# Recasting the scan of a hybrid RWKV-7 layer: row-half products, a written matmul order, a solve in pieces

## The chip, the cores and the metric

The kernel runs on one core of a Trainium2 chip. The metric is the device time of one execution in microseconds, as the median over runs; lower is better. The engines are TensorE (PE in the profile, with its weight loads as PEld), VectorE (DVE), ScalarE (ACT), GpSimd (POOL) and SyncE (SP), which issues the DMA transfers here.

## The reference, cut to what matters

One layer: a SwiGLU block, a token mixer, and a second SwiGLU block, each followed by a LayerNorm. 1152 tokens (128 of context, 1024 latent) of 1024 channels, in f32. The change touches the token mixer's recurrence, which runs forward and backward over the tokens for 16 heads of 64 channels:

```python
def _rwkv7_step(S, inp):
    r, w, k, v, kk, a = inp
    sa = jnp.einsum('dbhvk,dbhk->dbhv', S, kk)
    S = S * w[..., None, :] - sa[..., :, None] * (kk * a)[..., None, :] + v[..., :, None] * k[..., None, :]
    return S, jnp.einsum('dbhvk,dbhk->dbhv', S, r)
```

The outputs y of both directions are added, normalised over the 64 channels of each head (the group norm), joined by a bonus term, gated and projected. A second branch pools the tokens over windows, and two sigmoid gates weigh the branches. The final context states are an output too.

## The kernel before, in words

**The stages.** `tile_step` runs the first SwiGLU block; the input projection of the mixer with all that prepares the scan; the scan; then the output projections and the second SwiGLU block. The big products work on 384 tokens at a time with 128x128 weights, each value split into two fp32r parts, three matmuls for a product (`mm3`, lines 134 to 136). `Weights.get` loads a weight (line 122), ACT casts its high part (line 125), and DVE or POOL subtracts for the low part (line 127).

**The scan.** It treats 64 tokens as a chunk. The 18 chunks of 8 heads are a pass of 18 steps, the first two of context, and there are two passes (`hb`): 36 steps in `steps`. A step handles one chunk of the forward direction (d = 0) and one of the backward direction (d = 1) at once. Inside a step the recurrence becomes small f32 products, in `main(s)`:

- line 1015: the state times the chunk's keys and queries, into `xy`. Two heads share 128 partitions. The state is kept twice: `Sc`, plain, [128, 4, 64], and `Sb`, block diagonal, [128, 4, 128], so that one product with 128 rows serves two heads. One step has eight such products.
- line 1020: adds the masked products `LM` times the values, for the half of `xy` that holds x (d = 0 in partitions 0 to 63, d = 1 in 64 to 127).
- line 1024: ACT copies x to `Xs`, a half for each direction.
- line 1028: the inverse `W` of a triangular matrix times `Xs`; line 1032: ACT writes minus the result into `vu`, beside the values.
- line 1038: the update of the state, `sp`; line 1039 (DVE) adds it to `Sc`, line 1040 (POOL) multiplies by the decay, and lines 1041 and 1042 (ACT) copy the two halves into `Sb`.
- line 1046: the outputs y; line 1049 copies them to `yt`, and they go to a tile of the group norm or to memory.

Ahead of a step, `pre` loads its chunk `ak` (512 KB for a direction, three buffers), `pre_lm` computes the masks' products (line 987, one row half `e` at a time, four products of 64 rows, then a DVE multiply by the mask, line 988), and `pre_kb` transposes the keys (line 994).

**The solve.** `solve(i)` inverts the triangular matrices of four steps (two units). It loads them (lines 735 and 737), copies one of them transposed on ACT (line 739), runs 31 dependent pairs of DVE operations (lines 744 and 746), sends the result through memory to rearrange it (line 748 and after), transposes on DVE (lines 755, 758), and joins the 32-wide blocks by small matmuls (line 768, `ph`). The inverse is written to memory (`wi_d`, line 781) and read back by `load` into `W`. Solve 0 runs before the scan; the others start at every fourth step, for the unit two solves ahead; the head of a solve is emitted in one go, its four matmul parts one at a time.

**The filler.** The projections of the gates and of the pooling branch, 900 matmuls of 384 columns, are a generator, `filler`. Sixty of them (`AHEAD`) run before the first step; `fill(k)` emits the rest in five places of each step, in the shares of `SPREAD`.

**The group norm.** `group_norm(hb, tt)` is emitted when both directions of 128 tokens are there: a sum on POOL (line 1081), mean, subtraction, squares, variance, power and product on DVE, ACT and POOL (lines 1083 to 1091). `back` then transposes on TensorE (line 1096), scales on ACT (line 1100), adds the bonus on POOL (line 1101) and stores. The parts left at the end of the scan run inside the next stage, in `w_o`.

**What sets the order.** The compiler's scheduler orders the instructions of each engine by a simulated timeline, the earlier in the program the higher the priority. `tc.manual_schedule(engines=...)` keeps the program's order for the named engines instead; the opening, the ends of the SwiGLU blocks and the output projections have it for TensorE. In the scan before, the scheduler also orders TensorE, except that `tc.issue_after` holds the filler and the solve's matmuls behind a named matmul of the step.

Of the kernel before, what the change touches and what calls it, by code (L numbers as in the profile page):

```python
# [11 lines left out]
ALU = mybir.AluOpType  # L12
# [9 lines left out]
SPREAD = (7, 7, 6, 6, 0)  # L22
# [38 lines left out]
def tile_step(ctx: ExitStack, tc: tile.TileContext, I: dict, O: dict):  # L61
# [40 lines left out]
    wi_d = [dram.tile([P, 16, 64], F32, name=f"wi_{u}") for u in range(18)]  # L102
# [470 lines left out]
    with pool("mp", 4, psum=True) as psum, pool("ma", 2, psum=True) as paux, \  # L573
# [137 lines left out]
        gn = ctx.enter_context(pool("gn"))  # L711
# [9 lines left out]
        Wb = [sv.tile([P, 32, 64], F32, name="Wb0")]  # L721
        G.memset(Wb[0], 0.0)

        def solve(i, pps):
            def t4(nm):
                return sv.tile([P, 32, 32], F32, name=nm, tag="sv", bufs=4)
            Gq, Gt, Nt = t4("Gq"), t4("Gt"), sv.tile([P, 32, 32], F32, name="Nt")
            for k in range(2):
                u = 2 * i + k
                for d in range(2):  # L730
                    c0 = chunk0(u, d)
                    cb, cc, hb = c0 // 6, c0 % 6, u // 9
                    for hf in range(2):
                        p0 = d * 64 + hf * 32 + k * 16
                        S.dma_start((Gt if d else Gq)[p0:p0 + 16], qd_d[d][hb][cb][hf][:, cc:cc + 2].rearrange("a c e s t -> a (c e) (s t)"))
                    r0 = 96 * d
                    S.dma_start(Nt[r0:r0 + 32, k * 16:k * 16 + 16].rearrange("s (a n) t -> s a (n t)", a=4),
                                nd_d[d][hb][cb][:, :, cc:cc + 2].rearrange("s a c e t -> s a (c e t)"))
            A.copy(Gq[64:128], Gt[64:128].rearrange("p s t -> p t s"))
            Wd, pr = t4("Wd"), t4("pr")  # L740
            S.dma_start(Wd, I["id32"])
            for k in range(31):
# [3 lines left out]
                V.tensor_tensor(Wd[:, 0:k + 1, k + 1:32], Wd[:, 0:k + 1, k + 1:32], o, ALU.subtract)  # L746
            ed = dram.tile([2, 2, 32, 32, 32], F32, name="ed", tag="ed", bufs=2)
            S.dma_start(ed.rearrange("d b n i t -> (d b n) i t"), Wd)
            W = Wb[0]
            Dx = t4("Dx")  # L750
# [3 lines left out]
            DT = t4("DT")  # L754
# [4 lines left out]
            Mt = t4("Mt")  # L759

            def ph(jobs, k, after):
                pm = pps.tile([P, 16, 32], F32, name="ph", tag=TAGP[0])
                with ExitStack() as es:
                    if after is not None:
                        es.enter_context(tc.issue_after(after.ins))
                    for n in range(16 * k, 16 * k + 16):
                        for o, x, y in jobs(n):
                            PE.matmul(pm[o, n % 16, :], x, y, start=True, stop=True)
                return pm

            for k in range(2):
                ks = slice(16 * k, 16 * k + 16)
                after = yield
                pm = ph(lambda n: ((slice(32, 64), Nt[0:32, n, :], DT[0:32, n, :]), (slice(64, 96), Nt[96:128, n, :], Dx[96:128, n, :])), k, after)
                A.copy(Mt[32:64, ks], pm[32:64])
                A.copy(Mt[64:96, ks], pm[64:96])
                after = yield
                pm = ph(lambda n: ((slice(0, 32), Mt[32:64, n, :], W[32:64, n, 32:64]), (slice(96, 128), Mt[64:96, n, :], W[64:96, n, 0:32])), k, after)
# [4 lines left out]
        def solve_all(i, pps):  # L783
            g = solve(i, pps)
            next(g)
            for _ in range(4):
                advance(g)

        def advance(g, v=None):
            try:  # L790
                g.send(v)
                return True
            except StopIteration:
                return False

        TAGP = ["aux"]
# [6 lines left out]
        with pool("m2") as pl:  # L803
            solve_all(0, paux)
# [117 lines left out]
    with pool("s1") as pl, pool("spa", 2, psum=True) as psA, pool("spx", 2, psum=True) as psX, \  # L922
            pool("spg", 2, psum=True) as psG, pool("spm", 2, psum=True) as psM:
        maskLM = [sc[:, 0:128], sc[:, 128:256]]
        TAGP[0] = "m"
# [433 lines left out]
```

## Time and profile before

| | us |
|---|---|
| median of 3 runs | 3506.33 |
| lowest, highest run | 3505.05, 3511.2 |
| span of the profiled execution | 3503.5 |
| first to last matmul of line 1015 | 1660.6 to 2378.4 |

In the profile, a group of instructions stands as line, engine, operation, output tile <- input tiles, shapes and count, then busy time and mean duration in ns, then the engine's idle time just before them with what ended it. For a matmul, 64*128 is the part of the array that it uses: 64 rows and 128 columns. A timeline row has its start, its duration and the instructions that it merges. Matmuls overlap in the pipe, so the time that one costs is read from start to next start, not from its duration.

### The profile page before, as it was taken

What the parts mean: (1) busy time and instruction counts of PE and PEld (TensorE: products, weight loads), DVE (VectorE), ACT (ScalarE), POOL (GpSimd) and SP (SyncE); (2) the same over time, 40 slices, a digit from 0 to 9 for tenths busy, and PEclk for the clock granted to TensorE, in tenths of its full rate; (3) what the DMA queues carried; (4) which work ended last, traced back from release to release, by engine and by line L of the source; (5) the groups of instructions that cost most, each with busy time, mean ns of one, the idle gap of its engine ahead of it and who ended that gap; (6) DMA issues with size and microseconds to landing.
All of it is one profiled execution on the core that took longest, in us unless ns stands there. A gap on an engine that the chain in (4) does not pass through costs nothing. (4 is left out here: it accounts for less than half of the span.)

```text
span 3503.5 us, 61793 instructions
## 1 busy us (share of the span) xinstructions
PE 3325.9 (95%) x25166; PEld 3150.8 (90%) x25166; DVE 1962.7 (56%) x3237; ACT 1224.6 (35%) x2107; POOL 1348.6 (38%) x1077
## 2 busy tenths in 40 slices
PE   7999999999999999799999989998999999999997
PEld 7999999999988877598888888887999999999996
DVE  6888633357556788756365656534574332222466
ACT  4111111125534444532545555555345111111133
POOL 5111211136556666653322443157774111111144
PEclk9999999999999998799999989998999999999998
DMA  6443211123544545476557667665541111111133
GB/s 230 132 141 128 90 37 49 37 97 127 205 156 151 169 149 161 142 220 191 174 165 213 205 175 224 186 183 183 200 169 49 43 37 49 41 45 40 47 127 107
DMA packets 311421, 461.57 MB, mean 132 GB/s; under 512 B 115552, under 2 KB 211296, under 8 KB 309600
## 3 DMA queue, kind: packets, MB, share of 16 engines
q1 hardware_dynamic: 311136, 457.62, 41.1%
q8 instruction: 198, 3.24, 0.4%
q14 instruction: 87, 0.71, 0.1%
HBM read 325.44 MB, written 110.69 MB: 124 GB/s over the span
## 5 line engine op out<-in xcount | busy, mean ns | idle before, releaser
L127 POOL TENSOR_TENSOR wl<-wr,wh 128x1024 fp32r<-128x1024 f32 (+1 forms) x168 | 386.3, 2300 | 716.8 <-ACT wh L125 647.9
L125 ACT CAST wh<-wr 128x1024 fp32r<-128x1024 f32 (+1 forms) x321 | 321.9, 1012 | 829.8 <-PE po L135 424.0
L271 POOL TENSOR_TENSOR gl<-sg,gh 128x384 fp32r<-128x384 f32 x132 | 159.7, 1210 | 787.1 <-ACT gh L270 787.1
L134 PE MATMUL po<-gh,wh 128*128 128x384 f32 x1056 | 357.5, 339 | 8.5 <-ACT gh L270 4.2
L135 PE MATMUL pg<-h1l,wh 128*128 128x384 f32 x1056 | 356.4, 338 | 6.8 <-POOL h1l L143 6.8
L135 PE MATMUL po<-gl,wh 128*128 128x384 f32 x1056 | 357.3, 338 | 1.7 <-POOL gl L271 1.7
L136 PE MATMUL pg<-h3h,wl 128*128 128x384 f32 x1056 | 357.9, 339 | 0.0
L134 PE MATMUL pg<-h3h,wh 128*128 128x384 f32 x1056 | 357.6, 340 | 0.0
L134 PE MATMUL pg<-h1h,wh 128*128 128x384 f32 x1056 | 357.5, 339 | 0.0
L135 PE MATMUL pg<-h3l,wh 128*128 128x384 f32 x1056 | 356.8, 338 | 0.0
L136 PE MATMUL pg<-h1h,wl 128*128 128x384 f32 x1056 | 355.5, 337 | 0.0
L136 PE MATMUL po<-gh,wl 128*128 128x384 f32 x1056 | 355.5, 337 | 0.0
L127 DVE TENSOR_TENSOR wl<-wr,wh 128x1024 fp32r<-128x1024 f32 x153 | 223.2, 1463 | 214.8 <-ACT wh L125 214.7
L134 PE MATMUL pm<-h2h,wh 128*128 128x384 f32 x936 | 327.9, 350 | 8.5 <-ACT ga L810 5.1
L268 DVE TENSOR_TENSOR sg<-sg,pg 128x384 f32<-128x384 f32 x132 | 74.1, 561 | 464.9 <-PE pg L136 454.9
L135 PE MATMUL pm<-h2l,wh 128*128 128x384 f32 x936 | 328.3, 351 | 0.0
L136 PE MATMUL pm<-h2h,wl 128*128 128x384 f32 x936 | 328.3, 351 | 0.0
L288 DVE SCALAR_TENSOR_TENSOR ac<-po,modh,ac 128x384 f32<-128x384 f32 (+1 forms) x352 | 172.6, 515 | 95.4 <-PE po L136 95.4
L379 DVE SCALAR_TENSOR_TENSOR fm<-fm 128x512 f32<-128x512 f32 x224 | 183.8, 821 | 53.3 <-DMA fm<-in_w_mod 50.2
L134 PEld LDWEIGHTS po<-gh,wh 128*128 128x128 f32 x1056 | 199.2, 189 | 11.8 <-ACT gh L270 4.8
L135 PEld LDWEIGHTS pg<-h1l,wh 128*128 128x128 f32 x1056 | 200.3, 190 | 9.5 <-POOL h1l L143 8.9
L270 ACT CAST gh<-sg 128x384 fp32r<-128x384 f32 x132 | 67.5, 512 | 394.9 <-DVE sg L268 394.8
(289 smaller groups left out, 7681.3 us busy)
## 6 DMA issues: line engine op xcount, KB each, us to landing
wr<-in_ffn_in SPq DMA_DIRECT2D x120, 512.0 KB
ak<-ak SPq DMA_DIRECT2D x48, 768.0 KB
ak<-ak SPq DMA_DIRECT2D x72, 512.0 KB
wr<-in_w_mix SPq DMA_DIRECT2D x63, 512.0 KB
wr<-in_ffn_out SPq DMA_DIRECT2D x60, 512.0 KB
fm<-in_w_mod SPq DMA_DIRECT2D x112, 256.0 KB
sh<-pads SPq DMA_DIRECT2D x108, 130.0 KB
wr<-in_w_o SPq DMA_DIRECT2D x24, 512.0 KB
```

Of the source, the lines that this page charges most:

```text
L125: A.copy(h[:, :w], r[:, :w])
L127: e.tensor_tensor(l[:, :w], r[:, :w], h[:, :w].bitcast(F32), ALU.subtract)
L134: PE.matmul(ps, wh, xh, start=first and k == 0, stop=False)
L135: PE.matmul(ps, wh, xl, start=False, stop=False)
L136: PE.matmul(ps, wl, xh, start=False, stop=last and k == n - 1)
L268: lastv[0] = V.tensor_tensor(sg, sg, pu[:, :BN], ALU.mult)
L270: A.copy(gs[j, b][0][:, sl], sg)
L271: G.tensor_tensor(gs[j, b][1][:, sl], sg, gs[j, b][0][:, sl].bitcast(F32), ALU.subtract)
L288: lastv[0] = V.scalar_tensor_tensor(accs[b][:, n, s0:s1], po[:, s0:s1], modh[:, gate_i // 4, n, g:g + 1], accs[b][:, n, s0:s1], ALU.mult, ...
L379: V.scalar_tensor_tensor(jk, w, 1.0, silc[:, s, hf * 512:hf * 512 + 512], ALU.mult, ALU.mult, accum_out=part[:, kt, s, hf:hf + 1])
```

## The change

All of it is in the scan and what feeds it.

- **Row-half products.** `pre_lm` computes both row halves in one loop, alternating, into two PSUM tiles. The state product of `main` works in row halves too: sixteen products of 64 rows by 64 columns in place of eight.
- **Plain states.** `Sb`, its memsets and its copies are gone. `xy` is one tile of two banks, one bank for a row half, with both directions in each. The multiply by the decay moves from POOL to DVE. The copies of `Xs` and `vu` are split: d = 0 on ACT, d = 1 on DVE. The product with `W` gets a PSUM tile of its own (`us`).
- **Fixed matmul order.** The scan stands in `tc.manual_schedule(engines={PE.engine})`. Filler goes to three places in a step, in shares 6, 9, 10. `pre` loads three steps ahead instead of two.
- **The solve.** It is a generator of 18 parts, begun eight steps ahead, one part in each slot of a step; the DVE chain is cut into pieces of three pairs. Two tiles `Wb` in SBUF hold the inverses in turn; `wi_d` is gone. Solve 1's head runs before the scan.
- **Group norm in nine parts.** Each slot advances every group norm under way by a part. What is left at the end of the scan is drained there, inside the manual order; nothing is left for `w_o`. Its pool, with three buffers for y, moves into the scan's block.

```diff
-SPREAD = (7, 7, 6, 6, 0)
+SPREAD = (6, 9, 10)
...
-        Wb = [sv.tile([P, 32, 64], F32, name="Wb0")]
+        Wb = [sv.tile([P, 32, 64], F32, name=f"Wb{i}") for i in range(2)]
...
+            yield
             A.copy(Gq[64:128], Gt[64:128].rearrange("p s t -> p t s"))
...
+                if k % 3 == 2:
+                    yield
...
-                S.dma_start(wi_d[2 * i + k], W[:, ks])
...
-            solve_all(0, paux)
+            sol0, sol1 = solve(0), solve(1)
+            for _ in range(CHAIN + TAILS):
+                next(sol0)
+            for _ in range(CHAIN):
+                next(sol1)
...
-            pa = psA.tile([P, 4, P], F32, name="pa", tag="pa")
+            pa = [psA.tile([P, 4, P], F32, name="pa", tag="pa") for e in range(2)]
             for i in range(4):
-                PE.matmul(pa[:, i, :], ak[es, i, 128:256], ak[es, i, 0:128], start=True, stop=True)
-            V.tensor_tensor(c["LM"][s][d][:, :, e, :], pa, mk, ALU.mult)
+                for e in range(2):
+                    es = slice(e * 64, e * 64 + 64)
+                    PE.matmul(pa[e][:, i, :], ak[es, i, 128:256], ak[es, i, 0:128], start=True, stop=True)
+            for e in range(2):
+                V.tensor_tensor(LM[:, :, e, :], pa[e], mk, ALU.mult)
...
-                Sb = states[q, d][1]
-                for i in range(4):
-                    PE.matmul(xys[d][:, 2 * i:2 * i + 2, :], ak[d][:, i, 0:128], Sb[:, i, :], start=(i == 0), stop=False, skip_group_check=True)
+            xy = psX.tile([P, 2, 2, 4, 64], F32, name="xy", tag="xy")
+            for i in range(4):
+                for d in range(2):
+                    for e in range(2):
+                        es = slice(e * 64, e * 64 + 64)
+                        PE.matmul(xy[:, e, d, i, :], ak[d][es, i, 0:128], states[q, d][es, i, :], start=(i == 0 and d == 0), stop=False,
+                                  skip_group_check=True)
...
-                A.copy(Xs[x0:x1], xys[d][x0:x1])
+                (V.tensor_copy if d else A.copy)(eh(Xs[x0:x1]), xy[x0:x1, :, d])
...
-                A.mul(vu[d][x0:x1], xys[d][x0:x1], -1.0)
+                if d:
+                    V.tensor_scalar(vu[d][x0:x1], us[x0:x1], -1.0, None, ALU.mult)
+                else:
+                    A.mul(vu[d][x0:x1], us[x0:x1], -1.0)
...
-                G.tensor_tensor(Sc, Sc, PCst[:, d, cs[d], 4 * hb:4 * hb + 4].unsqueeze(2).broadcast_to([P, 4, 64]), ALU.mult)
-                A.copy(Sb[0:64, :, 0:64], Sc[0:64])
-                A.copy(Sb[64:128, :, 64:128], Sc[64:128])
+                V.tensor_tensor(Sc, Sc, PCst[:, d, cs[d], 4 * hb:4 * hb + 4].unsqueeze(2).broadcast_to([P, 4, 64]), ALU.mult)
...
+        LATER = (12, 14, 16, 19, 20, 22)
...
+        def slot_work(s, k):
+            for i in range(s // 4 - 1, s // 4 + 3):
+                at = 3 * (s - 4 * i + 8) + k
+                if i in sols and at in LATER:
+                    next(sols[i], None)
+                elif i > 1 and i < 9 and 0 <= at < 12:
+                    if at == 0:
+                        sols[i] = solve(i)
+                    next(sols[i])
+            drive(gns)
+
+        def between(s, k):
+            if k == 0:
+                if s + 3 < n:
+                    pre(s + 3)
+                if s + 1 < n:
+                    pre_lm(s + 1, 1)
+            slot_work(s, k)
             fill(k)
...
+        with tc.manual_schedule(engines={PE.engine}):
             for s in range(n):
                 if s == 18:
                     init_ctx(1)
-                if s % 18 == 2:
-                    init_lat()
-                after[0] = main(s)
+                main(s)
+                if s % 2 and s + 3 < n:
+                    load((s + 3) // 2)
                 if s + 1 < n:
                     pre_kb(s + 1, 1)
                 if s + 2 < n:
-                    pre(s + 2)
-                    pre_lm(s + 2, 0, 0)
+                    pre_lm(s + 2, 0)
+                slot_work(s, 2)
                 fill(2)
...
+            while gns:
+                drive(gns)
...
-                if n == 3:
-                    while backs:
-                        backs.pop(0)(paux, "aux")
```

The three slots of a step lie between line 1020's products and those with `W` (slot 0), between those and the state update (slot 1), and at the end of the step (slot 2).

More of the change, by code (lines that the diff above doesn't have):

```diff
@@ L710, in tile_step @@
         slctx.close()
-        gn = ctx.enter_context(pool("gn"))
         svctx = ExitStack()
@@ L719, in chunk0, with solve, t4 @@
             return 18 - 2 * j
-        Wb = [sv.tile([P, 32, 64], F32, name="Wb0")]
[L722 to L727, printed above, removed]
+        Wb = [sv.tile([P, 32, 64], F32, name=f"Wb{i}") for i in range(2)]
+        for t in Wb:
+            G.memset(t, 0.0)
+        def solve(i):
+            def t4(nm, tag_):
+                return sv.tile([P, 32, 32], F32, name=nm, tag=tag_)
+            Gq, Gt = t4("Gq", "gq"), t4("Gt", "pr")
             for k in range(2):
@@ L758, in solve, with ph @@
                 V.transpose(W[r, :, 32 * b:32 * b + 32], Dx[r])
[L759 to L768, printed above, removed]
+            yield
+            def ph(jobs, k):
+                pm = PPS[0].tile([P, 16, 32], F32, name="ph", tag=PPS[1])
+                for n in range(16 * k, 16 * k + 16):
+                    for o, x, y in jobs(n):
+                        PE.matmul(pm[o, n % 16, :], x, y, start=True, stop=True)
                 return pm
@@ L936, in init_ctx @@
             for d in range(2):
-                Sc, Sb = states[0, d]
-                G.memset(Sc, 0.0)
-                G.memset(Sb, 0.0)
-                S.dma_start(states[1, d][0], I["state"][d][:, 4 * hb:4 * hb + 4])
-        def init_lat():
-            for d in range(2):
-                Sc, Sb = states[1, d]
-                A.copy(Sb[0:64, :, 0:64], Sc[0:64])
-                A.copy(Sb[64:128, :, 64:128], Sc[64:128])
+                G.memset(states[0, d], 0.0)
+                S.dma_start(states[1, d], I["state"][d][:, 4 * hb:4 * hb + 4])
         ctxs = {}
@@ L967, in pre @@
             if s % 2 == 0:
-                load(u)
+                ctxs[u] = {"ak": {}, "LM": {}, "KBT": {}}
             hb, q, cs = steps[s]
@@ L1027, in main @@
                     x0, x1 = XR[d]
[L1028 to L1029 removed]
+                    last = PE.matmul(us[x0:x1, h, :], W[d][x0:x1, h // 2, h % 2, :], Xs[x0:x1, h, :], start=True, stop=True, skip_group_check=True)
+            between(s, 1)
             for d in range(2):
                 x0, x1 = XR[d]
[L1032 removed]
+                if d:
+                    V.tensor_scalar(vu[d][x0:x1], us[x0:x1], -1.0, None, ALU.mult)
+                else:
+                    A.mul(vu[d][x0:x1], us[x0:x1], -1.0)
             for d in range(2):
[L1034 removed]
+                Sc = states[q, d]
                 sp = psM.tile([P, 4, 64], F32, name="sp", tag="m")
@@ L1057, in main @@
                 ctxs.pop(u)
-            return last
         def other(tt, d):
@@ L1123, in fill @@
             quota[0] -= m
-            with tc.issue_after(after[0].ins):
-                for _ in range(m):
-                    next(fl, None)
-        def sol(s):
-            if sols and s >= sols[0][0]:
-                if not advance(sols[0][1], after[0]):
-                    sols.pop(0)
-        after = [None]
-        def between(s, k, last):
-            after[0] = last
-            if s + 1 < n:
-                pre_lm(s + 1, 1, k)
-            fill(k)
-            sol(s)
-        for _ in range(AHEAD):
-            next(fl, None)
-        with ExitStack():
+            for _ in range(m):
+                next(fl, None)
+        def slot_work(s, k):
[15 more added lines that the diff above has]
+            slot_work(s, k)
+            fill(k)
+        with tc.manual_schedule(engines={PE.engine}):
+            init_ctx(0)
+            for s in range(3):
+                pre(s)
+                if s % 2 == 0:
+                    load(s // 2)
+            for s in range(2):
+                for d in range(2 - s):
+                    pre_lm(s, d)
+                    pre_kb(s, d)
+            for _ in range(AHEAD):
+                next(fl, None)
             for s in range(n):
```

164 lines of the change are left out of this document (71 added, 93 removed).

## The prediction

> **What bounds the kernel now.** First the page, for the span and the share of each engine; then the windows view, cut at the first and last matmul of the scan; then the groups by line inside that window; then the timeline of TensorE.
>
> ```profile
> span 3503.5 us, 61793 instructions
> PE 3325.9 (95%) x25166; PEld 3150.8 (90%) x25166; DVE 1962.7 (56%) x3237; ACT 1224.6 (35%) x2107; POOL 1348.6 (38%) x1077
> ```
>
> ```profile
> 1660.00:2388.00 728.00, 682.82 (x9619) 611.29 (x9616) 380.53 (x771) 375.08 (x699) 261.39 (x230) 0.96 0.63 187
> 2388.00:2440.00 52.00, 40.27 (x191) 37.71 (x191) 29.15 (x39) 22.92 (x40) 45.05 (x32) 0.81 0.65 205
> 1810.00:1820.00 10.00, 5.78 (x70) 5.67 (x71) 4.17 (x13) 5.19 (x8) 1.23 (x2) 0.66 0.56 171
> ```
>
> The columns of a window are PE, PEld, DVE, ACT and POOL busy, then granted clock, DMA share and GB/s. The profiled span is 3503.5 us; the median of the three runs, 3506.33, lies 2.8 us above it, and I add that at the end. The scan is 36 steps in 728 us, 20.2 us a step, and TensorE is busy in 682.8 of them. So it is bound by TensorE's work and, for the other 45.2 us, by TensorE's waits. No other engine is above 380 us, and DMA is at 0.63. The window 1810:1820 shows that a wait costs twice: 4.2 us idle and a clock of 0.66. Over the scan the clock is 0.96, so 29 us of clock are missing, perhaps 20 of them under running matmuls. That makes 45 + 20 = 65 us of waits that something could recover; the rest must come from fewer or cheaper matmul passes.
>
> ```profile
> L987 PE MATMUL pa<-ak 64*128 64x128 f32 x1145 | 151.2, 290 | 6.1 <-DVE LM L988 6.1
> L744 DVE TENSOR_TENSOR pr<-Wd,Gq 128x31 f32<-128x31 f32 (+15 forms) x221 | 107.4, 486 | 64.8 <-ACT vu L1032 21.8 <-PE sp L1038 20.5 <-DMA Wd<-in_id 16.4
> L988 DVE TENSOR_TENSOR LM<-pa,sc 128x512 f32<-128x512 f32 x144 | 96.4, 684 | 113.1 <-PE pa L987 103.9 <-PE xy L1046 8.7
> L746 DVE TENSOR_TENSOR Wd<-Wd,pr 128x135 f32<-128x135 f32 (+15 forms) x222 | 95.5, 430 | 5.7
> L1015 PE MATMUL xy<-Sb,ak 128*128 128x128 f32 x576 | 79.7, 282 | 0.1
> L1038 PE MATMUL sp<-vu,KBT 128*64 128x64 f32 x1152 | 53.0, 240 | 16.1 <-ACT vu L1032 15.4 <-ACT yo L1100 0.6
> L994 PE MATMUL pt<-cst,ak 128*128 128x128 f32 x280 | 46.9, 293 | 14.5 <-DVE Sc L1039 14.4
> L1040 POOL TENSOR_TENSOR Sc<-Sc,PCst 128x256 f32<-128x256 f32 x71 | 45.3, 649 | 121.3 <-DVE Sc L1039 119.1 <-PE pt L994 2.2
> L1024 ACT COPY Xs<-xy 64x512 f32<-64x512 f32 x72 | 41.8, 581 | 57.2 <-PE xy L1020 56.4
> L1039 DVE TENSOR_TENSOR Sc<-Sc,sp 128x256 f32<-128x256 f32 x72 | 29.9, 417 | 70.7 <-PE sp L1038 68.2 <-ACT wh L125 2.0
> L1041 ACT COPY Sb<-Sc 64x256 f32<-64x256 f32 x71 | 28.7, 405 | 61.6 <-POOL Sc L1040 60.7
> ```
>
> The idle column of the PE rows says where the waits sit: 15.4 us for vu, 14.4 for the state sum, 6.1 for the masks. An f32 product is two passes here: 576 passes of line 1015 are 36 steps of eight products, and line 987 has 32 a step, 1152 in all, of which the trace kept 1145.
>
> **The row-half products.** What a pass costs, from the timeline of TensorE:
>
> ```profile
> 1716.18 2.05 PE L1015 MATMUL xy<-Sb,ak 128*128 128x128 f32 x16
> 1718.16 1.15 PE L1020 MATMUL xy<-vu,LM 64*64 64x64 f32 x32
> 1719.24 0.44 PE L854 MATMUL pm<-h2l,wh 128*128 128x384 f32 x1
> 1719.52 0.34 PE L856 MATMUL pm<-h2h,wl 128*128 128x384 f32 x1
> 1719.70 0.34 PE L852 MATMUL pm<-h2h,wh 128*128 128x384 f32 x1
> ...
> 1735.16 1.16 PE L1015 MATMUL xy<-Sb,ak 128*128 128x128 f32 x8
> 1736.25 0.91 PE L1020 MATMUL xy<-vu,LM 64*64 64x64 f32 x22
> ...
> 1828.06 1.16 PE L987 MATMUL pa<-ak 64*128 64x128 f32 x8
> 1829.15 1.43 PE L1028 MATMUL xy<-Xs,W 64*64 64x64 f32 x32
> ...
> 1831.94 1.71 PE L987 MATMUL pa<-ak 64*128 64x128 f32 x16
> 1833.58 0.63 PE L1038 MATMUL sp<-vu,KBT 128*64 128x64 f32 x14
> ```
>
> I read from start to next start. Sixteen state passes take 1.98 us, eight take 1.09: 0.111 us a pass, and 0.20 us left for the two changes of array shape around the group, 0.10 each. A lone group of eight mask passes also takes 1.09. Why 0.111? The modulation products of the opening answer:
>
> ```profile
> 30.74 1.93 PEld L481 LDWEIGHTS pmod<-cc,w 128*128 128x128 f32 x16
> 32.59 0.19 PEld L134 LDWEIGHTS pg<-h1h,wh 128*128 128x128 f32 x1
> ```
>
> They move two columns each and still need 1.85 us for 16, 0.116 a pass. So a pass with 128 weight columns is set by its weight load, however few columns move. This decides two things.
>
> *Masks (pre_lm).* Now one row half's four products, then the other's; in the change the halves alternate, into two banks. Do halves run side by side? In the 16-pass row the second half follows the first: at 0.111 that would be 16 x 0.111 + 0.20 = 1.98 us, and it took 1.64, so three passes were hidden where the halves meet. They overlap, weight loads too. Perfect pairs give 0.056 a pass. Line 1020, whose passes alternate between two quarter tiles, takes 1.08 for 32, less 0.10: 0.031 against 0.056 unpaired, a factor of 0.55 to 0.58, hence up to 0.064. I take 0.060: 1152 x (0.111 - 0.060) = 59 us less (54 to 63).
>
> *State product.* Before: 576 passes x 0.111 = 64 us, against a block-diagonal state. After: 1152 passes of half the rows and half the moving columns, but each still loads 128 weight columns: 1152 x 0.060 = 69 us. Halving the moved columns buys nothing; it is 5 us more (1 to 10).
>
> The Trainium skill, page "TensorE: Matmul & The Clock Gate", section "LDWEIGHTS (loading the stationary operand)", states the rule behind this: load time follows the columns, not the rows, 128 columns at 1.2 GHz, an estimate of 107 ns. The rows above agree (0.111). If such loads never overlapped, 1152 x 0.107 = 123 us would stand where I put 69.
>
> *Changes of shape.* From 1716.18 to 1735.16, one step, the timeline changes shape 17 times; the order written in the change has 10 or 11 a step. That step holds four groups of the solve, more than the mean, so I count three fewer of 0.10 us: 36 x 0.3 = 10 us less (5 to 18).
>
> TensorE's work: -59 + 5 - 10 = -64 us (-49 to -80).
>
> **Plain states and the split copies.** Gone are two ACT copies per direction and step (0.405 and as much again, 57 us of ACT) and the POOL multiply (0.649); a DVE multiply comes in, at 0.417 by the add beside it. The state chain after sp falls from 0.417 + 0.649 + 0.81 to 0.83 us a direction. Half of the Xs and vu work goes to DVE, 72 x 0.6 = 43 us (between ACT's 0.581 for it and DVE's 0.684 for a mask), with the multiplies 30: DVE rises from 380 to about 453 us. None of it is TensorE work; it shortens waits only.
>
> **Fixed order and the waits.** Line 1028 waits for Xs: 0.58 us plus hand-overs. Its cover is one mask group (0.96 + 0.2) and 840 x 6/25/36 = 5.6 filler passes at 0.175 (the three filler starts above): 2.1 us. The vu slot has 8.4 passes, 1.5 us plus 0.2 for changes, against 0.6. The state sum has line 1046, two transpose groups, a mask group and 9.3 passes, about 5 us, against 2. So each wait gets 1 us or more to spare. What makes them late now is this:
>
> ```profile
> 1811.63 1.92 ACT L739 COPY Gq<-Gt 64x1024 f32<-64x1024 f32 x1 [4.42 <-DMA Gt<-qd]
> 1813.57 1.21 ACT L1032 ACTIVATE vu<-xy 64x512 f32<-64x512 f32 x2
> ```
>
> ACT sat 4.4 us in the solve's first copy, waiting for its loads, with vu queued behind it, and TensorE idled. The change puts load and copy in different slots and starts eight steps ahead; but only TensorE's order is fixed, so the copy may still be queued too early. I keep 28 of the 65 us: -37 (0 to -65). Keeping the inverses in SBUF drops 18 writes and 18 reads of 512 KB from SP's queue; with DMA at 0.63 I count that at nothing. The reads of ak move from two to three steps ahead, past the pieces' loads on SP; what hides a late one is two whole steps.
>
> **The end of the scan.** The last two group norms now stand in TensorE's order ahead of everything in the next stage.
>
> ```profile
> 2388.02 0.34 PE L134 MATMUL pm<-gh,wh 128*128 128x384 f32 x1
> 2390.35 1.30 POOL L1081 TENSOR_TENSOR y<-y 128x512 f32<-128x512 f32 x1 [1.27 <-DMA y<-yt]
> ...
> 2413.36 1.04 POOL L1091 TENSOR_TENSOR y<-y,gvr 128x512 f32<-128x512 f32 x1
> ```
>
> Today the next stage starts at 2388.02, and the norms run beside it, from 2390.4 to 2414.4. After the change TensorE waits for them: some 18 us with POOL free of the next stage's work, 26 as now. Today 2388:2440 loses 12 us to idling and some 7 to the clock, mostly waiting for split tiles, which the new wait partly hides. I take +10 us (0 to +20).
>
> The Trainium skill, same page, section "Part 1: The HAM clock gate", puts the array at half rate after an idle window of 3.4 us and back after 3.4 busy ones; an estimate by it is 2 us within that term.
>
> **Sum.** -64 - 37 + 10 = -91: span 3412.5, run 3415 us. Ends: -80 - 65 + 0 = -145, 3361; -49 + 0 + 20 = -29, 3477.
>
> **Rivals.**
> (a) The waits stay as they are, since ACT and DVE are still queued ahead of late transfers: -64 + 10 = -54, 3452. For it: the Gq and vu rows above. Against: the cover of a microsecond or more.
> (b) The waits all but vanish and TensorE runs full: -64 - 60 + 5 = -119, 3387, or 3361 at the end of the terms.
> (c) DVE becomes the bound, and it ends slower. A piece of the solve is three pairs of lines 744 and 746: 3 x (0.486 + 0.430) = 2.75 us, in three slots a step for most of the first 28 steps. If in DVE's queue a piece and two masks (1.37) stand ahead of the copy of Xs or vu, the copy is ready at 2.75 + 1.37 + 0.6 = 4.7 us where TensorE has 2.1 or 1.7 to do: up to 2.6 us in some 54 slots, 140 us against a gain of 91, so 3555. It decides from 1.7 us a slot on. For it: DVE would be busy 453 / 36 = 12.6 us of a step of 17.4, more while the solves run. Against: pieces depend on nothing recent and can be queued earlier.
> (d) The halves do not overlap, as the load rule read strictly would have it: masks 0, state product +64, -10 - 37 + 10: +27, 3533. Against: the 1.64 us row.
> (e) The gains are offset by small in-order stalls, at weights or split tiles of the filler: about 3506.
>
> **How the numbers follow.** Forecast 0.47, (a) 0.22, (b) 0.16, (c) 0.08, (d) 0.04, (e) 0.03. The likeliest is 3415. The range 3355 to 3480 takes in its ends with (a) and (b) and leaves out the rest, 0.15. A measurement of this kernel tells about 0.2%, 7 us. Faster: 0.47 + 0.22 + 0.16 + a little of (e) = 0.87; within 0.2%: 0.03; slower: (c), (d) = 0.10, with the odd case of (e).
>
> **What would show it.** Right: sixteen mask passes in about 1.1 us; 32 state passes still near 2 us; scan near 630 us; idle for vu and the state sum below 10 us together; a gap before the first matmul of the next stage. Wrong: mask passes still 0.11 us apart (d); TensorE idle until a DVE copy of Xs or vu, in most steps (c); idle as large as now behind ACT (a); a state product well under 2 us, which would mean the load is not its bound.

## The result and the profile after

The changed kernel takes 3612.26 us (median of 4 runs, 3606.63 to 3619.64) against 3505.69 for the kernel before: 1.031 times as long, 95% interval 1.0288 to 1.0332. It is slower by 107 us where 91 us of gain were forecast.

The profiled spans, 3610.5 and 3503.5 us, differ by the same 107. Two marks divide them: the first matmul of the state product, and the start of the last matmul that adds to y.

| | before | after | difference |
|---|---|---|---|
| start to the first state product | 1660.6 | 1722.5 | +61.9 |
| the scan | 725.1 | 767.8 | +42.7 |
| from there to the end | 1117.8 | 1120.2 | +2.4 |

The page of the kernel after:

```profile
span 3610.5 us, 62643 instructions
PE 3276.3 (91%) x25742; PEld 3102.6 (86%) x25742; DVE 2047.3 (57%) x3381; ACT 1120.3 (31%) x1883; POOL 1299.7 (36%) x1002
```

TensorE works 50 us less than before and still ends later, so the loss is waiting. The windows view of the kernel after, with the columns of before, shows where:

```profile
1655.00:1722.00 67.00, 30.77 (x121) 25.01 (x120) 42.08 (x87) 16.42 (x25) 15.02 (x12) 0.57 0.51 150
1722.00:2003.00 281.00, 190.38 (x2836) 170.49 (x2836) 204.75 (x475) 70.98 (x111) 34.50 (x22) 0.81 0.42 130
2003.00:2489.00 486.00, 432.20 (x7204) 386.04 (x7206) 206.01 (x341) 183.22 (x337) 165.31 (x121) 0.90 0.52 152
```

The first row is the start: TensorE busy for 31 of 67 us, at a clock of 0.57. The second row is the first 10 steps, 28.1 us each, with VectorE at 205 of 281 us. The third is the other 26 steps at 18.7 us; the kernel before took 21.6 and 19.6. The groups by line inside the scan:

```profile
L973 PE MATMUL pa<-ak 64*128 64x128 f32 x1104 | 83.4, 292 | 0.0
L1004 PE MATMUL xy<-Sc,ak 64*128 64x64 f32 x1152 | 73.8, 279 | 0.0
L1020 PE MATMUL us<-Xs,Wb 64*64 64x64 f32 x1152 | 60.4, 256 | 74.9 <-DVE Xs L1015 37.9 <-ACT Xs L1015 36.9
L1033 PE MATMUL sp<-vu,KBT 128*64 128x64 f32 x1140 | 52.8, 258 | 42.4 <-DVE vu L1025 42.4
L1015 DVE COPY Xs<-xy 64x512 f32<-64x512 f32 x36 | 25.0, 695 | 77.4 <-ACT Xs L1015 76.8
L738 ACT COPY Gq<-Gt 64x1024 f32<-64x1024 f32 x5 | 9.6, 1922 | 49.7 <-DMA Gt<-qd 40.5 <-DMA Wd<-in_id 9.2
```

What a group of mask products and of state products costs, from start to next start in the timeline of TensorE:

```profile
2104.39 2.00 PE L1004 MATMUL xy<-Sc,ak 64*128 64x64 f32 x32
2106.32 1.15 PE L1010 MATMUL xy<-vu,LM 64*64 64x64 f32 x32
2107.40 1.16 PE L973 MATMUL pa<-ak 64*128 64x128 f32 x16
2108.49 0.44 PE L847 MATMUL pb<-u,wh 128*128 128x384 f32 x1
```

The 32 state passes take 1.93 us and the 16 mask passes 1.09, no more than was forecast. But TensorE now waits 74.9 us for Xs and 42.4 for vu. In the kernel before it had waited 15.4 for vu, and for Xs:

```profile
PE xy L1028 <- ACT Xs L1024: 4.0, 1, 4.0
```

The two halves run one after the other: in none of the 36 steps does VectorE's half of Xs start before ScalarE's is done, and the same holds for vu. So whatever delays ScalarE's half delays both. (The 76.8 us are VectorE's idle time in 15 steps before that; the copy waited for takes 0.58 us of it each time. What imposes the order, no run shows.) And ScalarE stands 40.5 us at the copy of Gq, for its loads.

Where the solve's chain runs, from the windows of line 742 alone:

```profile
1500.00:1600.00 100.00, 16.52 (x31) 0.97 0.65 198
1600.00:1700.00 100.00, 29.76 (x62) 0.76 0.49 148
1700.00:1800.00 100.00, 25.44 (x62) 0.74 0.38 114
1800.00:1900.00 100.00, 26.53 (x62) 0.85 0.43 136
1900.00:2000.00 100.00, 24.40 (x62) 0.78 0.44 138
2000.00:2100.00 100.00, 0.00 (x0) 0.90 0.47 141
```

The numbers in brackets are chain steps, 31 to a solve. All nine solves are through by 2000, step 10 of 36; as written, solve 8 begins at step 24. Only TensorE's order was fixed. On VectorE and ScalarE the compiler's scheduler had pulled the pieces forward. The timelines of ScalarE and of VectorE show what that does in one step, where each engine waits at one instruction and runs none of those behind it:

```profile
1905.20 1.92 ACT L738 COPY Gq<-Gt 64x1024 f32<-64x1024 f32 x1 [13.81 <-DMA Gt<-qd]
1907.14 0.62 ACT L124 CAST wh<-wr 128x512 fp32r<-128x512 f32 x1
1907.67 0.59 ACT L1027 ACTIVATE vu<-us 64x512 f32<-64x512 f32 x1
```

```profile
1895.88 0.54 DVE L887 TENSOR_TENSOR gt<-gt,pb 128x384 f32<-128x384 f32 x1
1907.15 0.19 DVE L742 TENSOR_TENSOR pr<-Wd,Gq 128x31 f32<-128x31 f32 x1 [10.73 <-ACT Gq L738]
...
1910.39 0.70 DVE L1025 TENSOR_SCALAR vu<-us 64x512 f32<-64x512 f32 x1
```

ScalarE idles 13.8 us at the copy of Gq, with vu queued behind it. VectorE idles 10.7 us for the same copy; its half of vu stands behind four pairs of the chain. The wait of TensorE for that half, 12.4 us, is the longest of the ten that make up the 42.4.

### The profile page after: what moved, and what is told of

It is laid out like the page before. It is cut to its first block, busy times and chain, and to the rows that moved or that the text cites. A ratio compares the mean times of both kernels' runs of the same rounds, so it can differ in the third digit from the quotient of the medians.

```text
span 3610.5 us, 62643 instructions
## 1 busy us (share of the span) xinstructions
PE 3276.3 (91%) x25742; PEld 3102.6 (86%) x25742; DVE 2047.3 (57%) x3381; ACT 1120.3 (31%) x1883; POOL 1299.7 (36%) x1002
## 4 chain that ended last, share of the span: by engine, by line
PE 34%; DVE 8%; DMA 5%; issue 2%; ACT 2%; POOL 2%; SPq 1%; ACTq 0%; DVEq 0%; POOLq 0%
PE pg L134 5%; PE pg L135 5%; PE pg L133 5%; PE po L134 2%; PE po L133 2%; PE po L135 2%; DVE pr L742 2%; DVE Wd L744 2%; DMA wr<-in_w_out 1%; PE pa L973 1%; PE sp L1033 1%; PE pm L134 1%; PE pm L133 1%; PE pm L135 1%; PE us L1020 1%
## 5 line engine op out<-in xcount | busy, mean ns | idle before, releaser
L133 PEld LDWEIGHTS pg<-h1h,wh 128*128 128x128 f32 x1056 | 201.2, 191 | 1.3 <-ACT h1h L141 0.8
```

The source lines that it names most:

```text
L133: PE.matmul(ps, wh, xh, start=first and k == 0, stop=False)
```

## The experiments

Each time is a median with its ratio to the kernel before on the same chip, and the interval. "Start" and "scan" are the stages of the table above, from each profile.

### Which part of the change

**act_copies**: the change with Xs and vu on ScalarE and the decay multiply on GpSimd, as before.

```diff
-(V.tensor_copy if d else A.copy)(eh(Xs[x0:x1]), xy[x0:x1, :, d])
+A.copy(eh(Xs[x0:x1]), xy[x0:x1, :, d])
```

> The changed kernel with DVE's new share undone: both halves of Xs and of vu are copied by ACT, and the decay multiply is on POOL again. Theory A (TensorE waits because these copies stand in DVE's queue behind the solve's chain): the waits for DVE's Xs (38 us), vu (42 us) and state (10 us) go, and some clock with them, so about 3520 us. Theory B (the fixed order of TensorE is what makes any late input cost): ACT's copies are late as well, and the gain is small, about 3590. Theory C (solves begun too early crowd the queues at the start): nothing at the start changes, about 3590.

3590.62 us, 1.026 (1.023 to 1.029); scan 743.5. VectorE's share of the copies and the multiply accounts for some 20 us of the 107 (22 by the medians, 18 by the ratios).

**free_order**: the change without the fixed matmul order in the scan; the filler is held behind the step's matmuls, as before.

> The changed kernel without the fixed order of TensorE in the scan: the scheduler orders it, with the filler held behind the named matmul of its place. Theory B: TensorE finds other work while an input is late, the scan's waits fall from 144 us to about 50, and the 60 filler matmuls ahead no longer stand before the first step; about 3500 us. Theory A: the steps wait for DVE all the same; at best the start is shorter by 30, about 3580.

3604.50 us, 1.030 (1.027 to 1.033). The start recovers to 1678.1, and the scan lengthens to 805.1. The order of TensorE by itself is not the cause, and a scan that starts 44 us earlier ends only 7 earlier.

**halves_only**: the kernel before with nothing but the alternating row halves.

> The kernel before with one part of the change alone: the mask products alternate between the row halves and go to two banks. By the prediction's price (1152 passes at 0.060 instead of 0.111) TensorE has 59 us less to do, and the changed kernel shows such passes at 0.058 a pass: about 3445 us if nothing else becomes the limit. If the waits of before simply grow into the gap, about 3480 to 3500.

3501.64 us, 0.9991 (0.9976 to 1.0007): no difference. The window from its first to its last state product, and the masks' group (151.2 us before):

```profile
1655.00:2379.00 724.00, 668.00 (x9482) 595.48 (x9479) 380.76 (x768) 368.32 (x685) 257.31 (x227) 0.93 0.63 185
L989 PE MATMUL pa<-ak 64*128 64x128 f32 x1140 | 127.9, 297 | 8.0 <-DVE LM L991 7.9
```

The masks' busy time fell by 23 us, not by 59, because in this kernel the scheduler orders TensorE, and the products written in alternation did not all run so:

```profile
1912.47 1.16 PE L989 MATMUL pa<-ak 64*128 64x128 f32 x8
1913.56 1.54 PE L1031 MATMUL xy<-Xs,W 64*64 64x64 f32 x32
...
1925.91 1.16 PE L989 MATMUL pa<-ak 64*128 64x128 f32 x16
1927.01 0.44 PE L852 MATMUL pb<-u,wh 128*128 128x384 f32 x1
```

Eight passes of one half take 1.09 us there, as long as sixteen alternating ones. About half of the passes (318 pairs of 576) start within 20 ns of their partner; in the changed kernel nearly all do (565). Of the 23 us little became time saved on TensorE: in the same window of the kernel before (1660 to 2378.4) it was busy 673 us of 718, here 668 of 724, with 11 us more idle time and a clock of 0.93 in place of 0.95. So the run tests the forecast's premise, that less work means less time, only in part. As far as it goes the premise fails: the cheaper masks shortened nothing.

**ahead_0**: the change with `AHEAD = 0`, so no filler ahead of the first step.

> The changed kernel with no filler ahead of the first step (AHEAD = 0); its 60 matmuls are spread over the steps. In the changed kernel they take 35 us ahead of the first state product, at half clock and waiting for split tiles. If that is what delays the scan by 62 us, the first step begins some 30 us earlier and the whole is about 3585 us. Theory C: the first step waits for the solves' DVE chain and loads anyway; about 3610, no change.

3638.41 us, 1.040 (1.037 to 1.043): the start is 29.6 us earlier and the scan 47.3 longer. The filler ahead of the first step is no loss; inside the steps it costs more.

### What the solve's chain costs

**chain_held**: each piece of the chain tied behind an instruction of its own step, so that the chain stands where it is written.

```diff
-                    next(sols[i])
+                    with tc.issue_after(hold[0].ins):
+                        next(sols[i])
```

> The changed kernel with each three-step piece of the solve's chain tied in VectorE's queue behind an instruction of the step that it was written in. Nothing else differs. Measured so far: in the changed kernel the first 10 steps take 28.1 us each (1722 to 2003) and the other 26 take 18.2 (2003 to 2475), and all 217 pairs of chain instructions of solves 2 to 8 stand in those first 10 steps, some 22 pairs a step, the copies of the step between them; as written there are 7.75 pairs a step over 28 steps. Theory D, the crowded chain: VectorE's queue delays the copies Xs and vu in the first 10 steps. Spread out, the first 10 steps fall to 19 to 21 us, the later ones rise by at most 2, and the time falls by 60 to 95 us, to about 3530 (3505 to 3555). Theory E, the late start and its loads slow the first steps, and the chain's place does not matter: 3600 or more. Theory F, more waits at the heads of the chains (they wait for the copy of Gq, 57.9 us in 6 waits) spread over all steps and cost the same: 3590 to 3620, but with even steps of about 21 us.

3592.78 us, 1.0248 (1.022 to 1.0276); scan 765.2, with 20.7 us a step in the first 10 and 21.5 after. My own theory, that crowding the chain into 10 steps was the cause, falls; theory F holds. Spread out, the chain costs nearly the same.

**no_chain**: the chain of solves 2 to 8 cut to one step (their inverses are left out).

```diff
-            for k in range(31):
+            for k in range(31 if i < 2 else 1):
```

> The changed kernel with the solve's chain cut from 31 steps to 1 for solves 2 to 8 (the inverses are therefore not computed; loads, round trip through memory, block products and everything else stay). It bounds what the chain can cost. Theory D: the first 10 steps at the later steps' 18.2 us give 3612 - 98 = 3515; a little less if the chain's end also held back the block products. Theory E (start and loads): 3595 or more. If it comes out far below 3515, the chain also slows the later steps through something else.

3535.86 us, 1.0081 (1.0058 to 1.0105); scan 683.2. So the chain, with the loads and copies that wait for it, costs about 76 us in the changed kernel.

**before_no_chain**: the same cut in the kernel before.

> The kernel before with the same part left out as in no_chain (the chain of solves 2 to 8 cut from 31 steps to 1, so their inverses are not computed). In the changed kernel that took 76 us off the time and 86 off the scan. Theory Q: the chain costs the kernel before nothing, because there the copies Xs and vu stand in ScalarE's queue and nothing urgent stands behind the chain: 3495 to 3510. Rival P: the chain paces the scan in both kernels, and what the changed kernel lost lies elsewhere: 3430 or less.

3496.35 us, 0.9984 (0.9966 to 1.0002). Here the chain costs nothing that can be told, 0.3% at most. So what costs time in the change is not the chain's work as such, but what stands behind it and behind its loads.

**held_free_start**: chain_held with the prologue ahead of the first step outside the fixed order.

> chain_held, and the prologue ahead of the first step (the first mask products, the first transposes, the 60 filler matmuls) taken out of the written matmul order, which begins with the first step. Theory D with the start as a cost of its own: the first state product goes from 1722 to about 1680 as it did without any written order, so 40 us under chain_held, about 3490. If the pace of the steps gives the saved start back (as it did in the runs without the order and without the 60 fillers), it comes within 10 us of chain_held, and the start was no cost of its own.

3591.91 us, 1.0241 (1.0217 to 1.0265). The start is at 1675.3, 35 us earlier, and the scan takes 789.2, 24 longer: the second reading of the expectation.

**held_act**: chain_held with the copies back on ScalarE.

> chain_held with both Xs and both vu copies on ScalarE and the decay multiply on GpSimd, as before the change. In the changed kernel that move alone brought 22 us. Theory D: those 22 us came from taking the copies out of the crowded queue, so with the chain spread little is left: within 10 us of chain_held. If the split over two engines is a cost by itself (VectorE's copy waits for ScalarE's), another 15 to 30 us below chain_held.

3578.71 us, 1.0202 (1.017 to 1.0234), 14 us below chain_held: at the edge of both readings, so little is decided.

### Where the chain's cost arises

**held_gq_late** and **held_act_gq_late**: chain_held and held_act with three empty parts between the solve's loads and the copy of Gq, and pieces of four steps.

```diff
-            yield
+            for _ in range(4):
+                yield
             A.copy(Gq[64:128], Gt[64:128].rearrange("p s t -> p t s"))
```

> chain_held with the copy of Gq and the chain begun three slots later after the solve's loads, in pieces of four steps, so that it ends in the same slot. In chain_held the matmuls of the state update waited 48.3 us in 6 waits, up to 12.8 each, for ScalarE's vu, and ScalarE stood at the copy of Gq, whose loads had not landed. Theory G, the urgent copy queued behind a copy that waits for a load: about 3548 (3535 to 3560). Rival H, VectorE's queue alone: 3580 or more, because four steps a piece stand ahead of Xs and vu instead of three.

> held_gq_late with the copies Xs and vu on ScalarE, the decay multiply on GpSimd. Theory G and the in-order queue of VectorE together: 3579 - 45 = about 3535 (3520 to 3550), 10 to 15 below held_gq_late. Rival: if ScalarE with all four copies becomes the pace, equal to or above held_gq_late.

3608.18 us, 1.0298 (1.0253 to 1.0343), and 3594.27, 1.0248 (1.0214 to 1.0283): both 15 us worse, where 45 less were expected. The runs missed what they were to test rather than refuting theory G: the empty parts bound nothing on ScalarE. In held_act_gq_late all six copies of Gq in the scan still stand between the copies of Xs and those of vu, and Gq waited 71.3 us in 5 waits, up to 16.8.

**held_act_gq_ak**: the same, with the loads of ak for the first three steps written ahead of the last projections.

> held_act_gq_late with the loads of ak for the first three steps written ahead of the last projections' loop instead of behind the loads of solve 2 (in the changed kernel TensorE waited 18.7 us for them). If the start is a cost of its own: the first state product at about 1690 instead of 1705, and 12 to 18 us below held_act_gq_late. If the 60 filler matmuls ahead of the first step still wait for their own inputs, the start stays where it is and nothing is won.

3578.94 us, 1.0215 (1.0178 to 1.0251): 15 us less, with the start 9 us earlier, at 1699.1, and the scan as long as before (758 us in both). So the late ak had cost some 9 us; the rest of the 15 lies behind the scan, and no run shows why. TensorE's waits in the steps of this kernel, and the timelines of ScalarE and TensorE in one step:

```profile
PE sp L1038 <- ACT vu L1032: 68.4, 6, 14.3
```

```profile
2043.60 1.17 ACT L1023 COPY Xs<-xy 64x512 f32<-64x512 f32 x2
2055.23 1.92 ACT L739 COPY Gq<-Gt 64x1024 f32<-64x1024 f32 x1 [10.47 <-DMA Gt<-qd]
2057.18 1.21 ACT L1032 ACTIVATE vu<-us 64x512 f32<-64x512 f32 x2
```

```profile
2044.82 1.14 PE L1028 MATMUL us<-Xs,Wb 64*64 64x64 f32 x30 [0.28 <-ACT Xs L1023]
...
2057.82 1.98 PE L1038 MATMUL sp<-vu,KBT 128*64 128x64 f32 x32 [9.42 <-ACT vu L1032]
```

The product with W is done at 2046.0 and vu could follow at once. It starts at 2057.2, because Gq stands ahead of it, and the load of Gt lands only at 2055.2. TensorE uses up its filler and then idles 9.4 us.

**tied_gq**: held_act_gq_ak with the copy of Gq five slots after its loads and tied behind the yt copies of that step on ScalarE; pieces of five steps; the transposes of the inverses two slots later, tied too.

```diff
-                    with tc.issue_after(hold[0].ins):
+                    with tc.issue_after(hold[0].ins), tc.issue_after(holdA[0].ins):
                         next(sols[i])
```

> held_act_gq_ak with the copy of Gq tied behind the yt copies of its step on ScalarE, five slots after the solve's loads (in the runs so far it stood between Xs and vu, right behind the loads), the chain in pieces of five steps, and the transposes of the inverses four slots after their loads, tied in the same way. Theory G, urgent copies queued behind copies that wait for a load: the 68.4 us of waits for vu in 6 waits fall to 15 or less and the 26 us for Sc to about 15, so 3579 - 60 = about 3520 (3505 to 3535). Rival H, the chain costs through VectorE's own work or the memory traffic: 3565 or more.

3514.76 us, 1.0023 (1.0007 to 1.0038); scan 690.4, which is 68 less than held_act_gq_ak and within 7 of the scan without the chain (the start is 8 us later again). The wait for vu has left the list of waits, whose head in the scan now reads:

```profile
PE us L1028 <- ACT Xs L1023: 43.9, 22, 5.9
PE pt L989 <- DVE Sc L1039: 30.1, 9, 8.0
```

and ScalarE no longer waits at the copy. All seven in the scan follow yt and KBT (the transposed keys) without idle time, as here:

```profile
1961.34 1.19 ACT L1048 COPY yt<-xy 64x512 f32<-64x512 f32 x2 [1.02 <-PE xy L1044]
1962.42 0.58 ACT L991 COPY KBT<-pt 128x512 f32<-128x512 f32 x1
1963.03 2.04 ACT L739 COPY Gq<-Gt 64x1024 f32<-64x1024 f32 x1
```

That is theory G: the scan shortened by as much as TensorE had waited for vu. Several edits went together here, so the times alone do not part them; the wait that vanished does. No run gave Gq and Gt a second buffer, so what that alone would bring is open.

**tied_gq_split**: tied_gq with Xs and vu split over ScalarE and VectorE, as in the change.

> tied_gq with the copies Xs and vu split between ScalarE and VectorE as in the change, the decay multiply on VectorE. VectorE's halves then stand behind chain pieces of five steps (5 x 2 x 0.42 = 4.2 us). If the split is a loss by itself: 20 to 40 us above tied_gq. If its serial copies were only slowed by the other waits: within 5 us.

3544.66 us, 1.0104 (1.0088 to 1.0119): 30 us above tied_gq. TensorE waits 31.5 us in 15 waits for VectorE's vu. In 8 of them vu stands behind pieces of the chain, in 7 behind the solve's transposes and mask products. The split is a loss by itself. Against the changed kernel this run differs by the ties, the later Gq and transposes, the pieces of five and the earlier ak: that is 68 us less. With the split undone, another 30, and 9 of the 107 are left.

### Beyond the cause

**tied_gq_free**: tied_gq with the prologue outside the fixed order.

> tied_gq with the prologue ahead of the first step taken out of the written matmul order, so that its matmuls can stand among those of the last projections. The start is a cost of its own: first state product at 1665 to 1680 instead of 1699, and 10 to 30 us below tied_gq, about 3500. Rival: the steps give it back, within 5 us.

3508.91 us, 1.0006 (0.9994 to 1.0018). The start is 34.5 us earlier, at 1672.7, and the scan takes back 15.6. In medians 6 us are left, with intervals that overlap.

**tied_gq_tail**: 108 filler matmuls kept for the group norms behind the scan.

> tied_gq with 108 of the filler matmuls kept back and written between the last parts of the group norms behind the scan, where TensorE waits 16 to 18 us for GpSimd's last multiply. 108 x 0.17 to 0.33 = 18 to 36 us of work would stand in those waits: 8 to 15 us below tied_gq. If the scan gives the same back: equal.

3561.76 us, 1.0153 (1.0138 to 1.0168): 47 us worse, a clear miss. The scan took 30 us longer without that filler (the wait of the transposes for the state sum went from 30 to 52 us), and the part behind it 18 longer. There the trace shows the added products standing ahead of the next stage rather than in its waits: that stage's first products of the normalised outputs (`pm<-yh`) start 49.1 us after the scan in place of 33.0, and the lag stays.

**tied_gq_cover** and **tied_gq_cover_xs**: tied_gq_free with the third slot's filler ahead of the transposes; then also `SPREAD = (9, 9, 7)`.

```diff
-                if s + 1 < n:
-                    pre_kb(s + 1, 1)
                 if s + 2 < n:
                     pre_lm(s + 2, 0)
                 slot_work(s, 2)
                 fill(2)
+                if s + 1 < n:
+                    pre_kb(s + 1, 1)
                 if s + 2 < n:
                     pre_kb(s + 2, 0)
```

> tied_gq_free with the order at the end of each step changed: the next mask products and the filler matmuls of the third slot stand ahead of the two groups of transposes, which in tied_gq_free waited 29.3 us in 10 waits for the state's addition (the PSUM tile they write into is the one that it reads). If these waits are the missing time: they go to 10 us or less and the time falls by 15 to 25, to about 3488. If something else sets the step's length: within 6 us of tied_gq_free, and the wait turns up elsewhere, most likely at vu or Xs.

> tied_gq_cover with the filler matmuls spread 9, 9 and 7 over the three slots in place of 6, 9 and 10, so that half as many again stand in the wait for Xs (38.3 us in 23 waits in tied_gq_free). If that wait is missing time: another 10 to 20 us, about 3475. If the step's chain is the bound, the wait for Xs shrinks and another grows: within 6 us of tied_gq_cover.

3495.34 us, 0.9972 (0.9956 to 0.9987), and 3494.38, 0.9975 (0.9957 to 0.9992). Both beat the kernel before, by about 0.3%. But that is not the scan's gain: in the profiles they reach the second SwiGLU block at 2633 and 2629 us, the kernel before at 2633, and some 6 us of the gain lie in that block, which the change does not touch (see below). Covering the state sum brought some 14 us, a little below what was expected; more filler for Xs brought nothing. In the scan of tied_gq_cover:

```profile
PE us L1028 <- ACT Xs L1023: 34.9, 16, 6.2
PE ph L774 <- DVE Sc L1039: 11.4, 5, 4.0
PE pt L989 <- DVE Sc L1039: 4.2, 3, 3.2
```

Half of the 29.3 us for the state sum is gone. Part of the rest moved on to the solve's matmuls.

## Why the prediction was wrong

In the prediction's terms the scan changed by -57 us of work and +99 us of waits, the start by +62, the stage behind the scan by +12, and the last block by -9: +107. The waits are the step that failed, and the start is a term that the sum did not have.

**"So it is bound by TensorE's work."** This premise failed too. In tied_gq, with the solve's waits gone, TensorE is busy 602.6 of the scan's 691 us, where 679.8 of 725 were before: 77 us less work, and a scan only 35 us shorter. halves_only points the same way on a smaller scale. A busy share of 94% over a stage did not make the engine its bound: what was taken from its matmuls came back, in large part, as idle time, at a lower clock (0.90 where it was 0.96).

```profile
1661.00:2386.00 725.00, 679.82 (x9587) 608.74 (x9587) 379.49 (x770) 372.83 (x694) 259.53 (x229) 0.96 0.63 187
1707.00:2398.00 691.00, 602.56 (x10081) 539.32 (x10080) 373.32 (x753) 303.45 (x522) 242.90 (x214) 0.90 0.55 163
```

The first row is the scan of the kernel before, the second that of tied_gq.

**Masks, -59 us: right.** 151.2 us of busy time became 83.4 for 1104 recorded passes, which is 87 for 1152. Sixteen passes take 1.09 us from start to next start; about 1.1 was to show it right.

**State product, +5 us: right in kind, too dear.** Thirty-two passes take 1.93 us where sixteen took 1.98, 2 us less over 36 steps, and busy time went from 79.7 to 73.8. Halving the moved columns bought next to nothing, as forecast, so the loads still set the price, and they overlap between the halves. The Trainium skill, page "TensorE: Matmul & The Clock Gate", section "LDWEIGHTS (loading the stationary operand)", has load time follow the columns; the estimate of 123 us, for loads that never overlap, which was rival (d), is not what the trace shows.

**TensorE's work in all, -64 (-49 to -80): right.** In the changed kernel TensorE is busy 623 of the scan's 768 us, 57 less than before. The changes of shape fell from 14.3 to 10.7 a step, where three fewer were counted.

**Waits, -37 us: the step that failed.** TensorE's idle time in the scan rose from 45 to about 144 us, +99. The text had named the mechanism and its row ("the copy may still be queued too early") and then counted a gain. It took "different slots" of the program for distance in the queue. The program's slots bind TensorE alone, and Gq and Gt had lost the buffers that let their loads run early: with one buffer each, a solve's loads start only when the chain of the solve before is done. The microsecond of cover in a slot could not hide a copy that stood up to 14 us at its loads. Leaving the chain out gave back 76 us; tying it and the copy of Gq behind other work, with ak loaded earlier, 68.

**The split copies, "it shortens waits only".** They lengthened them, since the halves run in turn: undoing the split is worth some 20 us in the change and 30 in tied_gq. The multiply by the decay, put at 0.417 us on VectorE, took 0.596 on average, since a few took up to 2.5 us, one of them while GpSimd ran a subtraction.

**Rival (c), slower by VectorE's queue, 3555, chance 0.08.** The result came out on its side, and its mechanism is real: copies of vu stood behind pieces of the chain. It left out the larger part, the copy of Gq that waits for its loads ahead of vu, and what late loads cost. The chances beside it were added up wrongly: (c) and (d) are 0.12, not 0.10.

**The start, not counted: +62 us.** The sum has no term for it. TensorE's waits from 1655 to 1722 in the kernel after:

```profile
PE pa L973 <- DMA ak<-ak: 18.7, 1, 18.7
PE pw L847 <- ACT us L898: 9.4, 3, 7.9
```

The loads of ak stand in SP's queue behind those of solve 2, which wait for solve 1's chain, and behind stores that wait for the pooling on GpSimd (14.1 us) and for a gate's result from ScalarE (5.6 us, right ahead of ak). The fixed order lets nothing else in ahead of them. Then the 60 filler matmuls take 35 us, where 60 at 0.175 would take 10, since the pooling products among them wait for their inputs and the fixed order holds the rest behind them. But an earlier start does not bring its 62 us: each run whose prologue was freed or emptied (free_order, ahead_0, held_free_start, tied_gq_free) had a longer scan, which took back 16 to 47 us.

**The end, +10 us: right.** The wait is there (17.9 us in two waits of the last transposes for GpSimd, against 18 forecast), and from the scan's end to the first matmul of the second SwiGLU block it takes 259.3 us in place of 247.3: 12 us longer. The +2.4 of the table hides this, because that block, which the change does not touch, takes 861.0 us in place of 870.4. So it does in every profile: 868 to 870 in kernels made from the one before, 861 to 864 in those made from the change. At a full clock in both, 200 us from its middle hold 1144 matmuls before and 1153 after; why, no run shows. So the small +2.4 is luck.

**What stays open.** With the solve's waits gone the scan is 690 to 706 us, where 624 would have matched the forecast. In tied_gq TensorE's work is as forecast or less, and 88 us are idle. Two waits make up most of the idle time, for Xs (43.9) and for the state sum (30.1). Covering the second helped by half; with more filler for the first, the wait did not shrink (34.9 and 33.9 us). I take the step's own chain, copy by copy, to be the bound there, but that is argued, not shown.

## What to carry to other kernels

Fixing one engine's order says nothing of the others: an instruction that waits for a load holds up every urgent one behind it in its queue, so tie it to a place where its load has landed. (A buffer that is free earlier may help too; no run tried it.) Before you count a saved matmul as saved time, take it out alone, see in the trace that it is gone, and see whether the stage shortens. Keep short urgent copies and a long chain of small operations on different engines.

## What the runs showed of the hardware

Products of 64 rows alternating between the two row halves of the array overlap their weight loads: sixteen passes with 128 weight columns take 1.09 us, where they took 1.64 one half after the other. Within a pair the second starts some 7 ns after the first, and the next pair 105 ns later. The sixteen loads take less than 1 us:

```profile
2067.87 0.97 PEld L973 LDWEIGHTS pa<-ak 64*128 64x128 f32 x16
```

The clock stayed at half after the start's wait, although TensorE was busy most of the time. Windows of the kernel after, from the first mask product on:

```profile
1674.00:1678.00 4.00, 3.12 (x20) 2.53 (x20) 3.69 (x11) 0.59 (x1) 0.00 (x0) 0.50 0.98 331
1678.00:1682.00 4.00, 3.19 (x18) 2.68 (x19) 3.83 (x10) 0.00 (x0) 0.00 (x0) 0.50 1.03 384
1682.00:1686.00 4.00, 3.31 (x20) 2.59 (x18) 3.86 (x9) 1.00 (x2) 1.00 (x1) 0.50 0.24 71
1686.00:1690.00 4.00, 4.00 (x16) 3.81 (x15) 3.83 (x10) 0.68 (x2) 0.00 (x0) 0.50 0.10 36
1690.00:1694.00 4.00, 1.97 (x8) 1.39 (x7) 3.79 (x7) 1.41 (x3) 2.08 (x2) 0.93 0.00 0
1694.00:1698.00 4.00, 2.62 (x7) 1.71 (x7) 3.76 (x8) 1.61 (x3) 2.00 (x2) 0.50 0.18 49
```

Twelve microseconds at 80% busy did not raise it. Behind four at 100% it rose, and after one window at half load it was lost again. So in this stage waits of 0.5 to 1.5 us went with half speed: most of the 60 filler matmuls cost 0.32 us from start to start, and 0.175 in the scan before. About 1.1 us of the busy time in each of the first windows are transposes; whether these count for the clock, no run here shows. The Trainium skill, same page, section "Part 1: The HAM clock gate", has full rate return after a sustained busy window of about 3.4 us; the rows agree, and in them 80% busy was not enough.
